# A hybrid attention and pooling layer on one Trainium2 core: the gate and pooled-channel projection by seven products of quarters in macro tiles 1 to 7, with x read already turned

## The chip, the cores and the metric

The kernel runs on one core of a Trainium2 chip, in one launch. The metric is the device time of that launch in microseconds (us). Before the change the median of 3 runs was 1232.03 us (1231.07 to 1233.27). Engines are named as in the profile: PE is TensorE (matrix products), PEld its weight loads, DVE is VectorE, ACT is ScalarE, POOL is GpSimd, SP is SyncE, whose queue issues all DMAs of this kernel.

## The reference, cut to what matters

x is 4096 tokens by 1024 channels, float32. One layer:

```
h    = RMSNorm(x) * pre_norm_g
q, k, v, g_a, u_p, g_p = split(h @ w_in)       # widths 512, 128, 128, 512, 512, 512
a    = banded_attention(q, k, v) * silu(g_a)   # 8 query heads, 2 key heads, |i-j| <= 128, bias, sink
p    = multiscale_pool(u_p) * silu(g_p)        # centred means over 2/4/8/16 tokens minus the token,
                                               # a 128x128 map per group of 128 channels, a scale
out  = x + RMSNorm([a ; p] @ w_out) * post_norm_g
```

The change is about the 1536 columns g_p, g_a and u_p of the product h @ w_in.

## The kernel before, in words

Every float32 operand of a large product is split into two float16 halves, high and low, and a product is taken as three: high by high, low by high, high by low. All three accumulate in the same PSUM bank. Weights are scaled by powers of two ahead of the split, which the gates' scale factors undo.

**Two stages.** Stage A projects g_p, g_a and u_p with tokens in the free dimension, stage B does all the rest: q, k, v, scores, softmax, values, the gated product, the output product by seven products of quarters (already so in both kernels), and the residual. Stage A ends where the first k projection starts (528.8 us in the profile).

**Stage A** goes over 8 macro tiles (m) of 512 tokens, each with 12 weight tiles (si) of 128 columns: 0 to 3 are g_p, 4 to 7 g_a, 8 to 11 u_p. One call of mm(m, si) (L593) is 24 matmuls: 8 blocks of 128 channels by 3, each with 128x128 weights and 512 moving columns. Its PSUM bank is one of three in turn (bank, L79). What follows a tile is set in after (L604): for a gate a sigmoid on ACT (L497), a multiply on DVE (L502) and, for g_a, a store to DRAM (L506); for u_p an evacuation on ACT (L515), edges of 8 tokens copied to and from the neighbour (L522, L523), and one macro tile later the pooled means: 1 to 4 dependent sums on DVE (L535), one more step (L551), the gate's multiply on POOL (L558) and a store.

**x** comes in token order in four blocks of 128 per macro tile (L157). The square sum goes to ACT (L163), the row scale to POOL (L172, L176), the high half to ACT (L185), the low half to DVE (L188). A DMA then turns the halves so that channels lie on partitions (x_turn, L195). The turned tiles are also stored (L200) and read back in stage B.

**Weights.** Each weight tile is loaded (L216), multiplied by the pre-norm gain on DVE (w_fold, L223), squared on ACT (L251), partly summed on POOL (w_presum, L257), summed over partitions by a product with ones on PE (w_norm, L266), scaled (scale_pow, L117 to L132, then the reciprocal at L275), and split on ACT (w_high, L281) and DVE (w_low, L285). A weight tile of u_p is first multiplied by the map of its pooling group: u_load (L227), u_prod on PE (L236), u_fold on DVE (L244). This happens in macro tile 0 for the 12 tiles of stage A. In macro tiles 1 to 3 it happens for the 6 tiles of q, k and v, two per macro tile. Macro tile 4 takes the norm of w_out, tiles 5 and 6 its split into quarters and their sums and differences (wo_sum1, wo_sum2, wo_high, wo_low; L443 to L483). Raw weights lie in 6 slots of 128x1024 float32.

**Order.** All instructions of a stage are put into a list by due(t, function, ...) with a due time t written by hand (L636) and are issued, on each engine's own queue, in the order of t, ties in the order of the list. The due times fix this order and nothing else: at run time each instruction waits for what it reads and for what it overwrites, and whatever stands behind it on its engine's queue waits too. Before the products of macro tile 0 six products of a tile of ones keep PE busy (warm_up, L576). The first two weight tiles of macro tile 0 go block by block as x arrives (mm_block, L586).

Lines that the prediction also uses: L371 (eight rows of attention bias scaled and masked on DVE), L599 (the products of mm), L847 (the q and k projection of stage B), L883 (scores), L981 (the v projection).

Of the kernel before, what the change touches and what calls it, by code (L numbers as in the profile page):

```python
# [17 lines left out]
P = 128  # L18
# [38 lines left out]
H_SCALE = 2.0**10  # L57
# [3 lines left out]
QKV_EVAC = 2.0**-14  # L61
U_EVAC = 2.0**-15
GP_EVAC = 2.0**-31
GA_EVAC = 2.0**-45
# [4 lines left out]
def hybrid_layer(ctx: ExitStack, tc, io, out):  # L69
# [22 lines left out]
    wb_h = const.tile([P, 6, KT, P], F16, name="wb_h")  # L92
    wb_l = const.tile([P, 6, KT, P], F16, name="wb_l")
    bias = const.tile([P, NH, 3 * P], F32, name="bias")
# [3 lines left out]
    cg = const.tile([P, 8], F32, name="cg")  # L98
    invc = const.tile([P, NH], F32, name="invc")
# [9 lines left out]
    x_scr = dram.tile([NM, P, BPM, 2 * KT, P], F16, name="x_scr")  # L109
    yp_scr = dram.tile([NB, P, 4, P], F32, name="yp_scr")  # L110
    ga_scr = dram.tile([NB, P, 4, P], F32, name="ga_scr")
    w_scr = dram.tile([8, P, 2, HK, 512], F16, name="w_scr")

    def scale_pow(dst, n2, floor, top):
# [17 lines left out]
        nc.vector.tensor_scalar(out=dst, in0=m4, scalar1=2.0**63, scalar2=None, op0=ALU.mult)  # L132


    xpool = ctx.enter_context(tc.tile_pool(name="xpool", bufs=1))


    with ExitStack() as actx:
# [4 lines left out]
        wa_h = pa1.tile([P, 12, KT, P], F16, name="wa_h")  # L143
        wa_l = pa1.tile([P, 12, KT, P], F16, name="wa_l")
        edge = pa1.tile([P, 4, 16], F32, name="edge")

        x_t, x_n, x_p, rs_t, w_t, n2_t, sq_t = {}, {}, {}, {}, {}, {}, {}
        pw = pa1.tile([P, 4, P], F32, name="pw")


# [4 lines left out]
        def x_load(b):  # L155
            x_n[b] = pa.tile([P, D], F32, name=f"xn{b}", tag="xn", bufs=4)
            nc.sync.dma_start(x_n[b], io["x"][b * P : (b + 1) * P, :])  # L157

        def x_square(b, eng=None):
            junk = pa.tile([P, D], BF16, name=f"jk{b}", tag="sq")  # L160
            rs_t[b] = pa.tile([P, 1], F32, name=f"ssq{b}", tag="ssq", bufs=4)
            if eng is None:
                nc.scalar.activation(junk, x_n[b], AF.Square, scale=X_SQ, accum_out=rs_t[b])  # L163
            else:
                eng.tensor_tensor_reduce(
                    out=junk, in0=x_n[b], in1=x_n[b], scale=X_SQ**2, scalar=0.0,
                    op0=ALU.mult, op1=ALU.add, accum_out=rs_t[b],
                )

        def x_scale(b):  # L170
            s = rs_t[b]
# [3 lines left out]
            rs_t[b] = pa.tile([P, 1], F32, name=f"rs{b}", tag="rs", bufs=4)  # L175
            nc.gpsimd.tensor_tensor(out=rs_t[b], in0=s, in1=mhalf, op=ALU.pow)  # L176

        def x_high(b):
            m, i = divmod(b, BPM)
            if i == 0:  # L180
                pool = xpool if m % 2 else pa1
                x_t[m] = pool.tile([P, BPM, 2 * KT, P], F16, name=f"xt{m}", tag="xt")
            tag, bufs = ("wraw", W_BUFS) if b in (2, 3) else ("xp", 2)
            x_p[b] = pa.tile([P, 2, D], F16, name=f"xp{b}", tag=tag, bufs=bufs)
            nc.scalar.activation(x_p[b][:, 0], x_n[b], AF.Copy, scale=rs_t[b])  # L185

        def x_low(b):
            nc.vector.scalar_tensor_tensor(  # L188
                out=x_p[b][:, 1], in0=x_n.pop(b), scalar=rs_t.pop(b), in1=x_p[b][:, 0],
                op0=ALU.mult, op1=ALU.subtract,  # L190
            )

        def x_turn(b):
            m, i = divmod(b, BPM)
            nc.sync.dma_start(  # L195
                x_t[m][:, i], x_p.pop(b).rearrange("p a d -> p (a d)"), transpose=True
            )

        def x_store(m):
            nc.sync.dma_start(x_scr[m], x_t[m])  # L200

        def x_block(b, t):

            due(t, x_square, b)
            due(t + 1.2, x_scale, b)
            due(t + 2.2, x_high, b)
            due(t + 3.4, x_low, b)
            due(t + 4.7, x_turn, b)


        gg = pa.tile([P, KT, P], BF16, name="gg", tag="yt")
        gb = g_pre.rearrange("p (k o) -> p k o", o=1).to_broadcast([P, KT, P])

        def w_load(si, src):
            w_t[si] = pa.tile([P, KT, P], F32, name=f"wraw{si}", tag="wraw", bufs=W_BUFS)
            nc.sync.dma_start(w_t[si], src)  # L216
# [5 lines left out]
        def w_fold(si, eng=nc.vector):  # L222
            eng.tensor_tensor(out=w_t[si], in0=w_t[si], in1=gb, op=ALU.mult)  # L223

        def u_load(j):
            w_t["u", j] = pa.tile([P, D], F32, name=f"wut{j}", tag="wraw", bufs=W_BUFS)
            nc.sync.dma_start(w_t["u", j], io["w_uT"][j])  # L227

        def u_prod(j, half):

            wt = w_t["u", j]
# [8 lines left out]
        def u_fold(j, half):  # L240
            if half == 0:
                w_t[A_U + j] = pa.tile([P, KT, P], F32, name=f"wu{j}", tag="wraw", bufs=W_BUFS)
            ks = slice(half * 4, half * 4 + 4)
            nc.vector.tensor_tensor(  # L244
                out=w_t[A_U + j][:, ks, :], in0=w_t.pop(("up", j, half)), in1=gb[:, ks, :],
# [3 lines left out]
        def w_square(si):  # L249
            sq_t[si] = pa.tile([P, KT, P], BF16, name=f"sq{si}", tag="sq")  # L250
            nc.scalar.activation(sq_t[si], w_t[si], AF.Square)  # L251
# [9 lines left out]
        def w_norm(si, n, by=None):  # L261

            sq = sq_t.pop(si)
            n2_t[si] = psa.tile([P, P], F32, name=f"n2_{si}", tag="n2")
            for k in range(n):
                nc.tensor.matmul(  # L266
                    n2_t[si], ones16 if by is None else by[:, k, :], sq[:, k, :],
                    start=(k == 0), stop=(k == n - 1),
                )

        def w_scale(si):
            scale_pow(sc[:, si : si + 1], n2_t.pop(si), 1e-20, W_SCALE)
# [1305 lines left out]
```

## Time and profile before

| | us |
|---|---|
| median of the runs | 1232.03 |
| span of the profiled execution, first to last instruction | 1229.4 |
| macro tile 0 of stage A | 0 to 92.6 |
| macro tiles 1 to 7 | 92.6 to 528.8 |
| stage B | 528.8 to 1229.4 |
| PE busy | 1203.6 |
| DVE busy | 826.3 |
| ACT busy | 633.6 |
| POOL busy | 380.6 |

The profile is that of one execution; the median of the runs lies 2.6 us above its span, which holds what surrounds the first and last instruction and the spread of runs. A page gives busy time per engine, a timeline of 40 slices, the queues, the chain that ended last and the costliest groups of instructions, each by line, engine, operation, tile names, shapes and count, with busy time and mean duration. "Idle before, releaser" is the time in which the engine stood still just before these instructions, and who ended it. Views of the trace give the same for a stretch of time, a line or a tile, or the instructions in order of time. Matmuls overlap in their pipeline, so the duration of one (379 ns for 512 columns) is longer than the distance from start to start.

### The profile page before, as it was taken

What the parts mean: (1) busy time and instruction counts of PE and PEld (TensorE: products, weight loads), DVE (VectorE), ACT (ScalarE), POOL (GpSimd) and SP (SyncE); (2) the same over time, 40 slices, a digit from 0 to 9 for tenths busy, and PEclk for the clock granted to TensorE, in tenths of its full rate; (3) what the DMA queues carried; (4) which work ended last, traced back from release to release, by engine and by line L of the source; (5) the groups of instructions that cost most, each with busy time, mean ns of one, the idle gap of its engine ahead of it and who ended that gap; (6) DMA issues with size and microseconds to landing.
All of it is one profiled execution on the core that took longest, in us unless ns stands there. A gap on an engine that the chain in (4) does not pass through costs nothing. (4 is left out here: it accounts for less than half of the span.)

```text
span 1229.4 us, 22327 instructions
## 1 busy us (share of the span) xinstructions
PE 1203.6 (98%) x8677; PEld 700.4 (57%) x8678; DVE 826.3 (67%) x1722; ACT 633.6 (52%) x1346; POOL 380.6 (31%) x385
## 2 busy tenths in 40 slices
PE   5999999999999999999999999999999999999998
PEld 4644444444444444476666765766676676667653
DVE  6665354545666564437778778777877877787786
ACT  5553333333435351136666755666575566667663
POOL 1233131313621211201244335424433533443331
PEclk9999999999999999999999999999999999999999
DMA  9473647496758783266957757765875676786594
GB/s 238 168 196 105 186 140 180 143 213 205 198 192 234 239 244 112 60 229 135 278 141 197 174 132 189 197 166 149 197 183 128 187 196 167 145 198 155 126 269 120
DMA packets 338986, 218.59 MB, mean 178 GB/s; under 512 B 267024, under 2 KB 309648, under 8 KB 335168
## 3 DMA queue, kind: packets, MB, share of 16 engines
q1 hardware_dynamic: 338880, 217.17, 65.9%
q8 instruction: 68, 1.11, 0.4%
q14 instruction: 38, 0.31, 0.1%
HBM read 94.43 MB, written 57.18 MB: 123 GB/s over the span
## 5 line engine op out<-in xcount | busy, mean ns | idle before, releaser
L599 PE MATMUL a<-xt,wa_h 128*128 128x512 f16 x1504 | 449.2, 379 | 0.1
L599 PE MATMUL a<-xt,wa_l 128*128 128x512 f16 x752 | 285.0, 379 | 0.0
L599 PEld LDWEIGHTS <-wa_h 128*128 128x128 f16 x1504 | 147.1, 98 | 175.9
L915 ACT ACTIVATE p<-p,nm 128x385 f32<-128x385 f32 (+1 forms) x256 | 153.0, 599 | 57.2 <-POOL p L898 37.9
L945 DVE SCALAR_TENSOR_TENSOR pn<-p,rd,pn 128x384 f16<-128x384 f32 (+1 forms) x256 | 156.5, 658 | 26.3 <-ACT pn L937 25.7
L847 PE MATMUL aq<-xt,wb_h 128*128 128x256 f16 x1024 | 173.1, 273 | 0.3 <-DVE mo L1182 0.3
L1154 PE MATMUL ms<-wo,ys 128*128 128x512 f16 x720 | 162.7, 379 | 1.5 <-ACT pn L937 1.5
L904 DVE CUSTOM_DVE_ANT_0 p<-s,bias,nsink 128x384 f32<-128x384 f32 (+1 forms) x256 | 155.9, 664 | 1.3 <-PE s L883 1.0
L937 ACT ACTIVATE pn<-p,rd 128x384 f16<-128x384 f32 (+1 forms) x256 | 136.3, 597 | 23.7 <-ACT p L915 21.2
L847 PE MATMUL aq<-xt,wb_l 128*128 128x256 f16 x512 | 139.5, 272 | 0.0
L847 PEld LDWEIGHTS <-wb_h 128*128 128x128 f16 x1280 | 125.2, 98 | 24.9 <-issue 9.3
L558 POOL TENSOR_TENSOR yt<-yt,s 128x512 f32<-128x512 f32 x32 | 51.5, 1608 | 256.9 <-DVE yt L551 148.2
L599 PEld LDWEIGHTS <-wa_l 128*128 128x128 f16 x752 | 73.5, 98 | 87.2
L1154 PE MATMUL m<-wo,y 128*128 128x512 f16 x540 | 119.7, 379 | 0.6 <-POOL y L1060 0.4
L1154 PEld LDWEIGHTS <-ys 128*128 128x128 f16 x720 | 69.1, 98 | 84.5 <-issue 4.2
L497 ACT ACTIVATE s<-a,cg 128x512 f32<-128x512 f32 x62 | 42.2, 684 | 145.3 <-PE a L599 140.8
L502 DVE SCALAR_TENSOR_TENSOR s<-a,s 128x512 f32<-128x512 f32 x62 | 42.4, 687 | 104.8 <-ACT s L497 104.8
L1188 POOL TENSOR_TENSOR mo<-mo,gpost 128x512 f32<-128x512 f32 x39 | 64.5, 1655 | 87.8 <-ACT jkb L1177 86.7
L1154 PEld LDWEIGHTS <-y 128*128 128x128 f16 x540 | 51.4, 98 | 65.3 <-issue 4.4
L188 DVE SCALAR_TENSOR_TENSOR xp<-xn,rs,xp 128x1024 f16<-128x1024 f32 x32 | 49.6, 1551 | 53.4 <-ACT xp L185 53.3
L883 PE MATMUL s<-k_all,q 64*128 64x384 f16 (+2 forms) x912 | 72.9, 296 | 2.8 <-ACT q L836 1.4
L1025 PE MATMUL o<-pt,vv 128*64 128x256 f16 x1128 | 68.2, 274 | 1.2 <-DMA pt<-pn 1.1
(159 smaller groups left out, 1589.2 us busy)
## 6 DMA issues: line engine op xcount, KB each, us to landing
xn<-in_x SPq DMA_DIRECT2D x32, 512.0 KB, 4.3
x_scr<-xt SPq DMA_DIRECT2D x7, 2048.0 KB, 7.4
xt<-x_scr SPq DMA_DIRECT2D x14, 1024.0 KB, 7.5
xr<-in_x SPq DMA_DIRECT2D x28, 512.0 KB, 4.1
out<-xr SPq DMA_DIRECT2D x28, 512.0 KB, 3.7
ga_scr<-s SPq DMA_DIRECT2D x32, 256.0 KB, 2.9
yp_scr<-yt SPq DMA_DIRECT2D x32, 256.0 KB, 2.3
w_scr<-wop SPq DMA_DIRECT2D x32, 256.0 KB, 2.6
```

The source lines that it names most:

```text
L188: nc.vector.scalar_tensor_tensor(out=x_p[b][:, 1], in0=x_n.pop(b), scalar=rs_t.pop(b), in1=x_p[b][:, 0], op0=ALU.mult, op1=ALU.subtract,)
L558: nc.gpsimd.tensor_tensor(out=t, in0=t, in1=g_t.pop((m, A_GP + j)), op=ALU.mult)
L599: nc.tensor.matmul(a3, w[:, si, k, :], x[:, :, kk, :], start=(n == 0), stop=(n == 3 * KT - 1))
L847: nc.tensor.matmul(a3, w[:, j, k, :], x[:, :, kk, :], start=(n == 0), stop=(n == 3 * KT - 1))
L883: nc.tensor.matmul(s_ps[:, gg, c0:c1], q_t[u, half][a, qi, jj, tl : tl + P], k_all[a, ki, kc : kc + c1 - c0], start=(n == 0 and c0 == 0), ...
L904: nc.vector.tensor_tensor_reduce(out=p_t[b, half][:, hh, :nk], in0=s_t[b, half][jj][:, gg, :nk], in1=bias[:, h, lo : lo + nk], scale=negc[ ...
L915: nc.scalar.activation(p[:, hh, : nk + 1], p[:, hh, : nk + 1], AF.Exp, bias=nm_t[b, half][:, hh : hh + 1], scale=-1.0, accum_out=den_t[b, ...
L937: nc.scalar.activation(prob_view(b, half)[:, 0, i], p_t[b, half][:, i, :nk], AF.Copy, scale=rd_t[b, half][:, i : i + 1],)
L945: nc.vector.scalar_tensor_tensor(out=pn4[:, 1, i], in0=p_t[b, half][:, i, :nk], scalar=rd_t[b, half][:, i : i + 1], in1=pn4[:, 0, i], op0= ...
L1025: nc.tensor.matmul(o_ps[a, 2 * half : 2 * half + 2], v[:, vi, kt, a], pt[b, half][:, pi, g, :, i, :], start=(n == 0), stop=(n == last),)
L1154: nc.tensor.matmul(z_t[u, tag], y[:, k, yi, :], wo[o][:, wi, k, :], start=(n == 0 and acc is None), stop=(n == 3 * HK - 1), skip_group_che ...
L1188: eng.tensor_tensor(out=mo, in0=mo, in1=gpost[:, cs], op=ALU.mult)
```

## The change: seven products of quarters, and x from a turned copy

**The product.** For each of the three groups q (QU for u_p, QP for g_p, QG for g_a) of four weight tiles, the product of 1024 channels by 512 tokens is taken by seven products of quarters (Strassen's scheme in Winograd's form). The quarters of x are two halves of the channels by two halves of the tokens, those of the weights two halves of the channels by two pairs of weight tiles. One product is 4 blocks of 128 channels x 3 (high, low) x 2 weight tiles = 24 matmuls with 256 moving columns; a macro tile takes 7 x 3 of them. Macro tile 0 still takes the plain product (mm, mm_block), its two weight tiles in blocks being 0 and 2.

**Sums.** From the turned x, four sums and differences of quarters per macro tile (x_sum), and eight casts to high and low halves, on ACT and DVE. From the weights, four sums per pair of weight tiles (t_sums on DVE, then t_high on ACT and t_low on DVE), made once, in macro tile 0 and at the start of macro tile 1. Weight tiles are now prepared in pairs (si, si + 2) with one scale for both: pair_scale waits for both norms.

**After a product.** Partial results are kept from PSUM on ACT (keep), joined to later ones on DVE (join), and gated (gates on ACT, gate_mult on DVE or POOL). One quarter leaves the bank directly (direct_u, direct_gates, direct_mult). The same three banks take five results in a row in each macro tile; two more banks take the second.

**x.** In macro tiles 1 to 7 x is read in token order for the square sums alone, and from a turned copy (an input that was there before, unused) for its values. The row scales go through DRAM to be spread over partitions (rs_row) and are multiplied in on DVE (y_scale). The DMA turns remain in macro tile 0 only.

**Moves.** The raw weight slots, the turned x and the weights of q, k, v share memory now, so the halves of q, k and v are stored and read back (wb_store, wb_load), and the attention bias and the post-norm gain are loaded late in macro tile 7, the bias rows (bias_head) following there on DVE instead of in macro tile 4. All scales drop by a factor of two. Stage B is otherwise as it was.

The due times of the steps for the attention weights and w_out keep their place as twelfths of a macro tile. The diff, cut to its core:

```diff
         for j in range(6):
             m, i, si = 1 + j // 2, 2 + 5 * (j % 2), SB + j
             also(m, i - 2, (0.2, w_load, si, io["w_b"][j]))
             also(m, i, (2.0, w_fold, si), (3.3, w_square, si), (4.4, w_presum, si))
             also(m, i + 2, ("norm", si))
+        def raw_put(key):
+            raw_free.append(w_t.pop(key))
+            if raw_wait:
+                raw_load(*raw_wait.pop(0))
+        def raw_load(key, src):
+            if raw_free:
+                nc.sync.dma_start(raw_get(key), src)
+            else:
+                raw_wait.append((key, src))
...
+        def t_sums(s1, eng=nc.vector):
+            r1, r2 = raw_of(s1), raw_of(s1 + 2)
+            b11, b21, b12, b22 = r1[:, :512], r1[:, 512:], r2[:, :512], r2[:, 512:]
...
+            minus(t1, b12, b11)
+            minus(t2, b22, t1)
+            minus(b11, b22, b12)
+            minus(b21, b21, t2)
+            raw_put(s1 + 2)
...
+        def t_low(s1, i):
...
+            if i == 1:
+                raw_put(s1)
...
+        STEPS = (
+            ("A11", 0, "p1"), ("A12", 1, "c11"), ("S2", 4, "u2"), ("S1", 2, "u4"),
+            ("S4", 3, "c12"), ("S3", 5, "c22"), ("A22", 6, "c21"),
+        )
+        def product(m, op, q):
...
+            for k in range(HK):
+                for wi, xi in ((0, 0), (1, 0), (0, 1)):
+                    for c in range(2):
+                        nc.tensor.matmul(
+                            acc[:, c], wa[:, q, wi, slot * HK + k, c * P : (c + 1) * P], x[:, xi, k, :],
+                            start=(fresh and n == 0), stop=(n > 3 * 2 * HK - 3),
+                            skip_group_check=True,
+                        )
+                        n += 1
...
+        def after(m, op, q, t):
+            what = STEPS[op][2]
+            if what in ("p1", "u2", "u4"):
+                due(t, keep, m, q, what)
+                return
...
+                    due(t, direct_gates, m, q)
+                    due(t + 1.0, direct_mult, m, q)
...
+            if q == QU:
+                if h == 0:
+                    due(t + 0.8, u_edges, m, n)
+                    if m:
+                        pooling(m - 1, 2 * n, t + 1.0)
+                        pooling(m - 1, 2 * n + 1, t + 2.0)
...
+        SLOT = 5.2
+        PT = 2.64
+        OP = 3 * PT
...
+        for si, s, n, f, h, l in (
+            (0, 9.25, 10.4, 10.7, 13.3, 14.5), (2, 10.3, 11.5, 11.9, 14.4, 17.1),
+        ):
+            due(s, w_square, si)
+            due(n, w_norm, si, KT, gg, 0)
...
+        due(11.0, row_prod)
+        due(11.4, warm_up)
...
+        pairs = [0, 1, 8, 9, 4, 5]
...
+            if n + 3 < len(pairs):
+                w = pairs[n + 3]
+                for i in range(2):
+                    if w >= A_U:
+                        due(now[0] + 0.2 + 0.1 * i, u_load, w - A_U + 2 * i)
...
         for m in range(1, NM):
-            for i, si in enumerate([8, 9, 10, 11, 0, 1, 2, 3, 4, 5, 6, 7]):
...
+            macro_x(m, t0)
+            for op in range(7):
+                for q in (QU, QP, QG):
+                    i = (3 * op + (QU, QP, QG).index(q)) * 12 // 21
...
+                    due(now[0], product, m, op, q)
+                    now[0] += PT
+                    after(m, op, q, now[0])
```

More of the change, by code (lines that the diff above doesn't have):

```diff
@@ L174, in x_scale @@
             )
[L175 to L185 removed]
+            nc.gpsimd.tensor_tensor(
+                out=r, in0=s, in1=mhalf if n == 1 else mhalf.to_broadcast([P, n]), op=ALU.pow
+            )
@@ new lines, in join, with gates @@
+        def join(m, q, b, part, n, h):
+            i = c_t[m, q, part]
+            c = cbig[:, i].rearrange("p (c t) -> p c t", c=2)
+            nc.vector.scalar_tensor_tensor(
+                out=dest(m, q, n, h) if q == QU else c, in0=acc_t[m, q, b], scalar=EV[q], in1=c,
+                op0=ALU.mult, op1=ALU.add,
+            )
+            if q == QU:
+                c_free.append(c_t.pop((m, q, part)))
+        def gates(m, q, part, n, h):
+            c = cbig[:, c_t[m, q, part]].rearrange("p (c t) -> p c t", c=2)
+            for i in range(2):
+                si = 4 * q + 2 * n + i
+                nc.scalar.activation(
+                    dest(m, q, n, h)[:, i], c[:, i], AF.Sigmoid, scale=cgs[:, si : si + 1]
+                )
@@ L730, in hybrid_layer @@
[L730 to L744 removed]
+        after0(0, 26.3)
```

832 lines of the change are left out of this document (569 added, 263 removed).

## Prediction

> **What bounds the kernel now.** I read the page first, then busy time by macro tile, then single instructions. The windows are macro tile 0, one ordinary macro tile (1 to 3 are alike), macro tiles 4 to 6, the last, and the attention stage with its start:
>
> ```profile
> span 1229.4 us, 22327 instructions
> ...
> 0.00:92.60 92.60, 79.37 (x565) 46.89 (x566) 59.16 (x133) 50.34 (x59) 21.81 (x31) 1.00 0.71 201
> ...
> 154.90:217.20 62.30, 62.30 (x293) 28.34 (x292) 29.43 (x50) 20.81 (x28) 14.45 (x16) 1.00 0.59 162
> ...
> 404.10:466.40 62.30, 62.30 (x290) 28.21 (x289) 37.09 (x50) 27.89 (x36) 11.12 (x12) 1.00 0.80 242
> 466.40:528.80 62.40, 62.40 (x291) 28.31 (x290) 26.51 (x52) 7.89 (x12) 10.39 (x10) 1.00 0.19 56
> 528.80:550.00 21.20, 18.88 (x202) 16.05 (x201) 8.03 (x24) 8.40 (x21) 0.19 (x1) 1.00 0.77 282
> 550.00:1229.40 679.40, 669.16 (x5886) 439.49 (x5883) 527.91 (x1185) 424.14 (x1068) 253.97 (x252) 1.00 0.69 174
> ```
>
> Columns: stretch, length, busy time of TensorE, weight loads, VectorE, ScalarE, GpSimd (with counts), granted clock, DMA share, GB/s. In macro tiles 1 to 7 TensorE is busy to the last hundredth and VectorE no more than 37.1 of 62.3: matmul columns set the time. Only macro tile 0 and the start of attention have gaps on TensorE. The span is 1229.4, the median of the runs 1232.0; I add the 2.6 between them at the end.
>
> **Term A, the products.** One projection tile (24 matmuls of 512 columns) and one pair of attention projections (48 of 256 columns, another weight each time, as in the new products), each alone:
>
> ```profile
> 66.43:71.61 5.18, 5.18 (x25) 2.26 (x24) 1.00 0.75 183
> 602.74:608.00 5.26, 5.26 (x48) 4.62 (x48) 1.00 1.13 239
> ```
>
> So 215.8 and 109.6 ns per matmul. A macro tile had 12 x 24 = 288, 62.16 us; it gets 7 x 3 x 24 = 504 of half the width, 55.23. Seven times 6.93 is **-48.5 us**. Weight loads are hidden at that rate in the second row. All else can only give this back.
>
> **Term B, macro tile 0.** It still runs the plain product, ten whole tiles after two in blocks, but prepares weights in pairs and builds four sums more of each pair. The order of instructions differs from the plan's intent in four places.
>
> ```profile
> 13.26 2.74 PE L576 MATMUL warm<-gg,ones 128*128 128x512 bf16 x6
> ...
> 28.69 2.02 PE L236 MATMUL wup<-pw,wut 128*128 128x128 f32 x16 [1.11 <-DMA wut<-in_w_uT]
> ...
> 35.73 0.38 PE L599 MATMUL a<-xt,wa_h 128*128 128x512 f16 x1
> ```
> ```profile
> 18.80 0.28 DVE L117 TENSOR_REDUCE m<-n 128x1 f32<-128x128 f32 x1
> ...
> 19.68 0.15 DVE L132 TENSOR_SCALAR sc<-m 128x1 f32<-128x1 f32 x1
> ...
> 37.98 1.28 DVE L285 SCALAR_TENSOR_TENSOR wa_l<-wraw,sc,wa_h 128x1024 f16<-128x1024 f32 x1
> 39.17 1.28 DVE L285 SCALAR_TENSOR_TENSOR wa_l<-wu,sc,wa_h 128x1024 f16<-128x1024 f32 x1
> ...
> 50.36 0.68 DVE L244 TENSOR_TENSOR wu<-wup,g_pre 128x512 f32<-128x512 f32 x1
> 50.96 0.15 DVE L275 RECIPROCAL isc<-sc 128x1 f32<-128x1 f32 x1
> ```
> ```profile
> 49.88 1.15 ACT L281 ACTIVATE wa_h<-wu,sc 128x1024 f16<-128x1024 f32 x1 [0.61 <-DVE sc L132]
> 51.80 1.06 ACT L251 ACTIVATE sq<-wu 128x1024 bf16<-128x1024 f32 x1 [0.76 <-DVE wu L244]
> ```
> ```profile
> 22.42 5.90 SPq L195 DMA_TRANSPOSE xt<-xp  x1
> ```
> ```profile
> DMA to landing us min/median/max: 4.4/5.5/7.9
> ```
> ```profile
> DMA to landing us min/median/max: 4.1/5.1/6.7
> ```
>
> The last two are the turned x blocks and the weight loads of the pooled channels. VectorE's pitch is 1.20 us at 1024 elements and 0.60 at 512, a scale takes 1.03 from its reduction to sc.
>
> First, the norm of weight tile 2 (w_norm) is queued behind the warm-up, which ends at 16.0, and the common scale needs it: scale at 18.1, high half 19.3, where the first block began at 15.8. The split of x blocks 2 and 3 queues behind, so the last turn is issued at about 26.9 instead of 22.4, lands at 32.4, and two blocks of a quarter tile (1.3 each) end at 35.2. Second, the six weight slots are full: the load of pooled tile 1 (u_load) waits until VectorE's sums of pair 0 (t_sums) free one, that of tile 3 until a low half of those sums (t_low) is done, and that low half stands behind the fold of tile 1 (u_fold) on VectorE, which needs the product (u_prod) of the first load. In a row: gates and low halves 3.0, fold 0.6, sums 1.9, load 5.1, half a product 1.0, fold and low half 1.2, load 5.1, product 2.0: 20 us. The first whole tile starts at about 55, not 35.7. Ten tiles (51.8) and norms (2.2) remain. Third, the norm of tile 10 stands behind the last product of pair 1, so tile 8 waits for scale, high and low half: 3.9. Fourth, VectorE has 54 us of work in the remaining 63, in order (20 sums and 20 low halves of 512 elements 24.0, 8 low halves of 1024 9.6, folds, scales and gates 13.5, x of macro tile 1 7): I count 5.4 more where tile 4 waits for its second load (1.6), tile 5 for its low half behind x's scaling (2.5) and tile 7 for the bank that the gate of tile 4 frees (1.3). End at 118.5 against 92.6: **+26**. Bounds: +17 with two loads at 4.1 and only the load chain and tile 8 counted, +32 with loads at 6.7 and a turn at 7.9.
>
> By the Trainium skill ("TensorE: Matmul & The Clock Gate", Part 1), an idle window of some 3.4 us halves TensorE's clock until it has been busy as long; the warm-up row agrees, 457 ns each against 215.8. No run here shows a pause of that length later; if the gaps between the pooled products do it, the sum would grow by an estimated 2 us.
>
> **Term C, norms of the attention weights in macro tiles 1 to 3.** Two per macro tile. On VectorE the fold (w_fold) comes after both pooled tiles (pool_tile) of its half, then the square on ScalarE, where the next gates are queued behind it, two partial sums on GpSimd and the norm on TensorE, where the next product is queued behind it.
>
> ```profile
> 353.69 0.71 DVE L535 TENSOR_TENSOR ws<-u 128x527 f32<-128x527 f32 x1
> 354.44 0.71 DVE L535 TENSOR_TENSOR ws<-ws 128x525 f32<-128x525 f32 x1
> 355.18 0.69 DVE L551 SCALAR_TENSOR_TENSOR yt<-ws,u 128x512 f32<-128x512 f32 x1
> 355.79 1.22 DVE L476 TENSOR_TENSOR wop<-wo_b,wop 128x1024 f16<-128x1024 f32 x1
> ```
> ```profile
> L257 POOL TENSOR_TENSOR sq<-sq x23: 669/1149/2051, 29.9 to 258.9; 128x512 bf16<-128x512 bf16 x13, 128x256 bf16<-128x256 bf16 x10
> ```
>
> A dependent sum has a pitch of 0.75, the last step 0.61. The second chain of a macro tile starts 1.2 after the first product of operand S4: pooled tiles 2 and 3 take 2.85 + 3.6, fold 1.2, square 1.1, partial sums 1.15 + 0.67 and hand-overs 0.2: 12.0. TensorE reaches the norm after three products, 7.9: it waits 4.1. The first chain (pooled tiles 0 and 1, 1.4 + 2.1) waits 0.9. GpSimd's gate of the one pooled tile also meets VectorE's sums of the other:
>
> ```profile
> 350.02 1.65 POOL L558 TENSOR_TENSOR yt<-yt,s 128x512 f32<-128x512 f32 x1 [19.07 <-DVE yt L551]
> 350.58 1.64 DVE L447 TENSOR_TENSOR wt<-wo_b,wt 128x512 f32<-128x512 f32 x1
> ```
>
> Beside it 1.64 instead of 0.69. I take half of that 0.95 per chain: 3 x (4.6 + 1.4) = **+18**; bounds +10 (pooled sums at a pitch of 0.60, no meeting) and +26 (each met, partial sums at 2.05).
> The Trainium skill ("SBUF — State Buffer", Who interferes with whom) says that a VectorE instruction with two inputs in SBUF and a GpSimd instruction that reads SBUF lock each other out for a whole instruction; the two rows agree. By its full price the sum would be 3 us higher here.
>
> **Term D, PSUM banks.** Each of three banks takes five results in a macro tile; TensorE may write again 5.3 us after a result is complete. After S4 the gate's multiply (direct_mult) on VectorE frees the bank, queued behind both pooled tiles: 1.2 + 6.4 + 0.7 = 8.3 against 7.9 in macro tiles 4 and 7. In 5 and 6 two subtractions and a low half of w_out (wo_sum1, wo_low) stand between, 2.5 more by the rows above: 2.9, with half a meeting 3.4 each. Together **+8**, bounds +2 and +13. ScalarE's keeps have slack.
>
> **Term E, x.** Reading x already turned takes 28 turns off SP's queue, and 28 splits off VectorE and ScalarE; TensorE had not waited for them, so that is worth 0. Added are four loads per macro tile (2 MB; the DMA share was 0.59 to 0.80) and the row of x's scales: written to DRAM, waited for on SP's queue with the last two loads queued behind it, read back broadcast. At about the loads' 4.1 us each way it takes 8 us, which is what lies between its due time and its use; squares that come late on ScalarE (C) delay it by 1 to 3. **+2**; 0, or +9 if it delays every chain of C and D.
>
> **Term F, start of attention.** Eight bias rows and the last pooled tiles now end on VectorE after the projection:
>
> ```profile
> L371 DVE SCALAR_TENSOR_TENSOR bias<-bias,invc,mask 128x384 f32<-128x384 f32 x8 | 7.9, 982 | 0.0
> ```
> ```profile
> 528.56 0.38 PE L599 MATMUL a<-xt,wa_h 128*128 128x512 f16 x1
> ...
> 540.23 0.28 PE L883 MATMUL s<-k_all,q 64*128 64x256 f16 x2 [0.75 <-ACT q L836]
> ```
>
> Scores began 11.4 us after the last product's pitch. From 6.9 before the end VectorE has 7.9 for bias, 9.9 for pooled tiles, 3.1 for joins and gates, then 1.4 for k, v and q: 15.4 after the end. **+4**, 0 to +6. Later stages keep instructions and order: 0.
>
> **Sum**: -48.5 + 26 + 18 + 8 + 2 + 4 = +9.5; span 1239, time **1241**. All low bounds together: -19.5; all high: +37.5.
>
> **Rivals.** *Faster:* VectorE's queue is ahead wherever TensorE is late, so only the load chain and the barest chains are left: +17, +10, +2, 0, +2 against -48.5, time 1214. It decides when the waits sum to under 46. For it speaks that VectorE's work still fits: per macro tile 16 passes over 1024 elements of x (19.5 at 1.22), 14 joins and gates of 512 (9.1), pooled tiles (10) and 7 to 15 for weights, 46 to 53 of 55 us; against it, that each chain starts from a product of its own macro tile, so an earlier queue doesn't shorten it. *Much slower:* every meeting with GpSimd at its full price (C +21, D +9) and the high bounds of B and E: -48.5 + 32 + 21 + 9 + 9 + 4, time 1258; VectorE is then the bound. For it speaks the 1.64 row, against it that the sums of L535 took 0.706 at the median, 2.736 at most:
> ```profile
> L535 DVE TENSOR_TENSOR ws<-ws x48: 694/706/2736, 104.7 to 511.9; 128x525 f32<-128x525 f32 x24, 128x521 f32<-128x521 f32 x16, 128x513 f32<-128x513 f32 x8
> ```
>
> *All hidden, as the due times say:* macro tile 0 ends at 90.5; 1185. The order of the loads speaks against it.
>
> **How the numbers follow.** Forecast 0.60 (1229 to 1252), faster rival 0.22, much slower 0.13, all hidden 0.05. The range 1212 to 1258 leaves out about 0.17. About 0.2% (2.5 us) is what a measurement tells from no change. Faster is the rivals' 0.27 less the part of the first near zero, 0.25; same 0.09, from the edges of the first rival and the forecast; slower 0.66.
>
> **What would show it.** First whole tile at about 55 and macro tile 1 at about 118; TensorE idle before the pooled products until the loads land; idle before norms in macro tiles 1 to 3, released by GpSimd, some 4 us in each second half and none in 4 to 7; a few us behind VectorE's gate multiply in 5 and 6; products at 2.63. Wrong if the first whole tile starts before 46 or if the norms are never waited for.

## The result, and the profile after

The changed kernel takes **1364.13 us** (median of 4 runs, 1361.21 to 1366.89) where the kernel before takes 1232.02 (4 runs, 1231.07 to 1233.27): a ratio of 1.107, 95% interval 1.105 to 1.109. The prediction said slower, 1241 us, range 1212 to 1258. The sign was right, and the size was missed by 123 us.

First the page of the changed kernel: the span, TensorE's line and the granted clock in 40 slices of 34 us.

```profile
span 1365.0 us, 25715 instructions
...
PE 1198.0 (88%) x10186; PEld 867.8 (64%) x10186; DVE 979.2 (72%) x1800; ACT 706.4 (52%) x1524; POOL 393.8 (29%) x363
...
PEclk9788989989897979889999999999999999999999
```

TensorE was busy 1203.6 us before and is busy 1198.0 now, although it has 48.5 us less to do, and its clock is no longer full in the first half of the span (each digit is a slice's granted clock in tenths, 9 for 90% or more). The next view has stretches as in the prediction: macro tiles 1 to 7, one a row, then the rest.

```profile
138.90:218.70 79.80, 61.08 (x509) 51.96 (x509) 56.25 (x74) 32.64 (x55) 16.06 (x12) 0.89 0.52 170
218.70:293.40 74.70, 59.12 (x511) 51.18 (x509) 48.06 (x61) 29.10 (x51) 17.21 (x13) 0.91 0.47 153
293.40:368.60 75.20, 59.28 (x510) 51.29 (x508) 47.80 (x61) 29.02 (x51) 17.20 (x13) 0.91 0.42 144
368.60:443.50 74.90, 59.95 (x508) 51.56 (x506) 44.29 (x68) 33.55 (x56) 28.76 (x17) 0.89 0.54 177
443.50:521.60 78.10, 60.09 (x506) 51.32 (x505) 55.98 (x68) 35.74 (x56) 11.20 (x9) 0.89 0.56 182
521.60:599.80 78.20, 60.46 (x506) 51.45 (x505) 56.15 (x61) 36.64 (x58) 12.02 (x9) 0.89 0.54 179
599.80:657.00 57.20, 55.38 (x506) 49.34 (x505) 36.03 (x47) 16.95 (x34) 11.15 (x8) 1.00 0.58 174
```

The columns are those of the prediction's first view: stretch, length, busy time of TensorE, weight loads, VectorE, ScalarE and GpSimd, granted clock, DMA share, GB/s. The last macro tile is what the products alone are worth: 57.2 us, TensorE busy 55.4, clock 1.00. It is also the only one that prepares no x for a next one. Each of the six others takes 75 to 80 us: 15 to 19 us of idle TensorE and 4 to 6 us more of busy time at a clock of 0.89 to 0.91. Macro tile 1 starts at 138.9 where the prediction had 118.5. The last product of stage A ends at 656.5 (before 528.8), and all that follows it takes 708.5 us (before 700.6).

The waits between 138 and 660 us (engine, line, releaser: us in total, times, longest) name who stood still for whom:

```profile
DVE ybig L279 <- DMA rb<-rs_scr: 75.8, 6, 17.9
...
PE n L389 <- POOL sq L376: 35.9, 6, 10.0
...
PE cl L902 <- ACT u L950: 32.5, 6, 7.1
...
PE cl L902 <- DVE gp L962: 24.2, 4, 7.8
```

VectorE waits once in each of macro tiles 1 to 6 (and once in macro tile 0) for the row of x's scales, which goes through DRAM (rs_row, L257 and L259; y_scale, L279). One macro tile in order of time shows how that reaches TensorE. First GpSimd, SyncE's queue, VectorE and ScalarE in macro tile 5, which starts at 443.5 (the time in brackets is the engine's idle time before the row and who ended it):

```profile
469.09 0.37 POOL L200 TENSOR_SCALAR ssq<-ssq 128x4 f32<-128x4 f32 x1 [2.54 <-ACT jk L191]
```
```profile
470.61 0.36 SPq L257 DMA_DIRECT2D rs_scr<-ssq  x1
479.47 0.33 SPq L259 DMA_DIRECT2D rb<-rs_scr  x1
```
```profile
473.55 1.23 DVE L687 TENSOR_TENSOR raw<-raw 128x1024 f16<-128x1024 f32 x1 [1.16 <-ACT raw L683]
484.85 2.36 DVE L279 TENSOR_TENSOR ybig<-ybig,rb 128x1024 f32<-128x1024 f32 x2 [10.07 <-DMA rb<-rs_scr]
...
494.53 0.70 DVE L775 TENSOR_TENSOR ws<-u 128x527 f32<-128x527 f32 x1
...
501.38 0.69 DVE L791 SCALAR_TENSOR_TENSOR yt<-ws,u 128x512 f32<-128x512 f32 x1
501.99 2.35 DVE L654 TENSOR_TENSOR raw<-raw 128x512 f32<-128x512 f32 x2
504.27 1.21 DVE L687 TENSOR_TENSOR raw<-raw 128x1024 f16<-128x1024 f32 x1
505.40 0.68 DVE L962 SCALAR_TENSOR_TENSOR gp<-ch,gp 128x512 f32<-128x512 f32 x1
```
```profile
486.11 1.04 ACT L285 CAST xt<-ybig 128x1024 f16<-128x1024 f32 x1 [6.00 <-DVE ybig L279]
491.27 1.15 ACT L651 ACTIVATE raw<-raw,rowsc 128x1024 f32<-128x1024 f32 x1 [4.12 <-DMA raw<-in_w_out]
...
493.26 0.59 ACT L950 ACTIVATE u<-ch 128x512 f32<-128x512 f32 x1
```

Then TensorE in the same stretch:

```profile
493.90 4.48 PE L902 MATMUL cl<-xt,wa 128*128 128x256 f16 x24 [6.58 <-ACT u L950]
506.13 15.65 PE L902 MATMUL cl<-xt,wa 128*128 128x256 f16 x120 [7.75 <-DVE gp L962]
521.62 8.02 PE L902 MATMUL ch<-xt,wa 128*128 128x256 f16 x72
```

The write of the row is issued 27 us after the start of the macro tile, not 20 as its due time says (x_loads at 1, the row 19 later), because the squares on ScalarE (L191) are late: GpSimd's row scale waits for the last of them. Its read can be issued only 8.9 us later and lands 5.4 us after that. VectorE is held for 10 us; the scaled x, the pooled tiles and the gate's multiply (L962) stand behind it in this order. ScalarE's cast of that x waits too, and behind it, with 4.1 us more of waiting for a load of w_out, stands the evacuation of the bank (direct_u, L950). So TensorE pauses twice, 6.6 and 7.8 us, and its first products behind each pause run slowly: 24 matmuls in 4.48 us, where such a row at full speed takes 2.78.

### The profile page after: what moved, and what is told of

It reads as the page before. It is cut to its first block, busy times and chain, and to the rows that moved or that the text cites. A ratio compares the mean times of both kernels' runs of the same rounds, so it can differ in the third digit from the quotient of the medians.

```text
span 1365.0 us, 25715 instructions
## 1 busy us (share of the span) xinstructions
PE 1198.0 (88%) x10186; PEld 867.8 (64%) x10186; DVE 979.2 (72%) x1800; ACT 706.4 (52%) x1524; POOL 393.8 (29%) x363
## 5 line engine op out<-in xcount | busy, mean ns | idle before, releaser
L902 PEld LDWEIGHTS <-wa 128*128 128x128 f16 x3528 | 357.0, 101 | 123.5 <-issue 71.2
L902 PE MATMUL ch<-xt,wa 128*128 128x256 f16 x2016 | 224.3, 273 | 7.3 <-ACT cbig L914 5.1
L1305 PEld LDWEIGHTS <-raw 128*128 128x128 f16 x1920 | 186.8, 98 | 39.5 <-issue 9.6
L902 PE MATMUL cl<-xt,wa 128*128 128x256 f16 x1008 | 135.4, 304 | 56.7 <-ACT u L950 32.5
L1374 ACT ACTIVATE p<-p,nm 128x385 f32<-128x385 f32 (+1 forms) x256 | 153.0, 599 | 57.2 <-POOL p L1357 38.0
L1305 PE MATMUL aq<-xt,raw 128*128 128x256 f16 x1536 | 173.1, 273 | 0.0
L1363 DVE CUSTOM_DVE_ANT_0 p<-s,ybig,nsink 128x384 f32<-128x384 f32 (+1 forms) x256 | 155.9, 665 | 1.4 <-PE s L1342 1.1
L279 DVE TENSOR_TENSOR ybig<-ybig,rb 128x1024 f32<-128x1024 f32 x28 | 33.4, 1221 | 88.3 <-DMA rb<-rs_scr 83.9
L1649 POOL TENSOR_TENSOR mo<-mo,ybig 128x512 f32<-128x512 f32 x39 | 64.8, 1661 | 87.5 <-ACT jkb L1638 86.3
L285 ACT CAST xt<-ybig 128x1024 f16<-128x1024 f32 x56 | 57.9, 1036 | 61.0 <-DVE ybig L279 48.1
L290 DVE TENSOR_TENSOR xt<-ybig,xt 128x1024 f16<-128x1024 f32 x56 | 69.5, 1249 | 14.7 <-ACT xt L285 14.7
L848 PE MATMUL a<-xt,wa 128*128 128x512 f16 x240 | 59.3, 406 | 18.4 <-ACT wa L425 16.8
```

The lines of the kernel that those rows point to most:

```text
L290: eng.tensor_tensor(out=o[:, w, 1], in0=y_view(i), in1=o[:, w, 0], op=ALU.subtract)
L848: nc.tensor.matmul(a3, weight(si, wi, k), xt[:, 0:2, k // HK, xi, k % HK, :], start=(n == 0), stop=(n == 3 * KT - 1),)
L902: nc.tensor.matmul(acc[:, c], wa[:, q, wi, slot * HK + k, c * P : (c + 1) * P], x[:, xi, k, :], start=(fresh and n == 0), stop=(n > 3 * 2 ...
L1305: nc.tensor.matmul(acc, w[:, j, k, :], x[:, k // HK, a, k % HK, :], start=(n == 0), stop=(n == 3 * KT - 1),)
L1363: nc.vector.tensor_tensor_reduce(out=p_t[b, half][:, hh, :nk], in0=s_t[b, half][jj][:, gg, :nk], in1=bias[:, h, lo : lo + nk], scale=negc[ ...
L1374: nc.scalar.activation(p[:, hh, : nk + 1], p[:, hh, : nk + 1], AF.Exp, bias=nm_t[b, half][:, hh : hh + 1], scale=-1.0, accum_out=den_t[b, ...
```

## The experiments

Theory 1: the row of x's scales is late and holds VectorE's queue. Norms, banks and x all come late by it, and the pauses drop TensorE's clock. Theory 2: the chains of norms and banks (terms C and D) are dear by themselves. Theory 3: the products of half width lower the clock by themselves. Times below are of one run each (the kernel before gave 1231.6 to 1232.2 beside them); differences are taken to the changed kernel's 1364.1 where no other kernel is named. The four runs of the changed kernel lie up to 5.7 us apart, so a difference of that size between two single runs tells nothing by itself.

### e1_no_row: no row through DRAM

```diff
-            nc.sync.dma_start(rs_scr[m].rearrange("(b p) -> p b", p=P), rs_t[m][:, 1])
-            rb_t[m] = pa1.tile([P, T], F32, name=f"rb{m}", tag="rb")
-            nc.sync.dma_start(
-                rb_t[m], rs_scr[m].rearrange("(o t) -> o t", o=1).to_broadcast([P, T])
-            )
+            rb_t[m] = rb_one        # set to 1.0 once, ahead of stage A
```

> The row of x's scales is not written to DRAM and read back; VectorE multiplies the turned x by a tile of ones that is set once (leaves out the scaling of x by rows in macro tiles 1 to 7). All else is as in the changed kernel, whose VectorE waited 84 us for the read of that row, seven times. Theory 1 (the row is late and holds VectorE's queue, so that norms, banks and x all come late, and the pauses drop TensorE's clock): no pause of TensorE over 5 us in macro tiles 1 to 6, its busy time per macro tile back from 59 to 61 to about 55.5, macro tiles 1 to 6 at 57 to 60 us each instead of 75 to 80, macro tile 0 about 12 us shorter: 1240 us (1230 to 1255). Theory 2 (the chains of norms and banks are dear by themselves, the row only fills idle time of VectorE): above 1330 us. Theory 3 (the clock drops because of the new products themselves, not because of pauses): pauses go but TensorE stays busy 59 to 61 us per macro tile: about 1270 us.

Measured **1298.3 us**: 65.8 less. Stretches of macro tiles 1, 2, 6 and 7:

```profile
130.20:200.80 70.60, 58.47 (x509) 50.92 (x509) 56.03 (x74) 32.69 (x55) 16.02 (x12) 0.95 0.56 188
200.80:265.30 64.50, 57.11 (x510) 50.37 (x508) 47.83 (x61) 29.03 (x51) 17.18 (x13) 0.97 0.51 172
...
465.80:531.80 66.00, 57.01 (x507) 49.94 (x506) 56.24 (x61) 36.65 (x58) 12.03 (x9) 0.97 0.64 208
531.80:588.40 56.60, 55.31 (x506) 49.28 (x504) 35.47 (x46) 16.96 (x34) 11.14 (x8) 1.00 0.59 176
```

This kernel leaves out the scaling of x. Macro tile 1 starts at 130.2, 8.7 sooner, and each of the six macro tiles is 8 to 12 us shorter. So the row costs 66 us, half of what was missed, and theory 1 holds for that half; the other half is still there. Its waits, by line (two lines higher than in the changed kernel: the norm L387, the gate's multiply L960):

```profile
PE n L387 <- POOL sq L374: 25.1, 6, 5.6
PE cl L900 <- DVE gp L960: 20.2, 4, 7.2
```

### e2_row_sooner and e11_row_sooner_base: the same with the row kept

```diff
-            x_loads(m + 1, t + 1.0)
+            x_loads(m + 1, t - 17.0)                          # e2
+            x_loads(m + 1, t - (19.0 if m > 1 else 9.0))      # e11, squares, scale and row 2 us further behind their loads
```

> The loads of x in rows, their squares, the scales and the row through DRAM are planned 18 us sooner for macro tiles 2 to 7 (that of macro tile 1 as it was); nothing is left out. Theory 1: VectorE waits for the row only once (8 us in macro tile 0), macro tiles 1 to 6 at 57 to 60 us each: 1255 us (1245 to 1270). Theory 2: within 15 us of the changed kernel's 1364. Theory 3: about 1285 us.

> The first edit of e4_pool_later alone: the row of x's scales sooner, pooled tiles and norms as in the changed kernel. Theory 1: like e2_row_sooner without its late start of macro tile 1: 1310 us (1303 to 1319), so that e4_pool_later's order of pooled tiles gave 12 us of its own.

Measured **1319.4** and **1312.9 us**. In e11_row_sooner_base VectorE waits for the row once, 7.0 us in macro tile 0, as theory 1 says (us and times, from the view of the tile rb):

```profile
  DMA rb<-rs_scr: 7.0, 1
```

Reading x sooner is enough to hide the round trip, and 51 us come back, although SyncE's queue still waits 63.1 us for the seven writes (63.5 in the changed kernel). So it is VectorE's wait that costs, not the wait on SyncE's queue. The 14.6 us left to e1_no_row lie in the start of macro tile 1 (7.6 later) and in macro tile 1 (7.0 longer). Theory 1's 1255 for e2_row_sooner was wrong for the reason that e1_no_row shows; nor did the milder shift remove the late start of macro tile 1 (TensorE still waits 7.5 us there for VectorE's multiply at L740, 9.4 in e2_row_sooner).

### e3_norm_later: the norms two products later

```diff
-            also(m, i + 2, ("norm", si))
+            also(m, i + 4, ("norm", si))
```

> The norms of the attention weights in macro tiles 1 to 3 stand two products later on TensorE's queue (their scale, halves and store with them); the row of x's scales stays as in the changed kernel. Theory 1: the pauses of 2.2 to 2.5 us in the first halves go (7 us in all), those of 9 to 10 us in the second halves only change their name, to a wait for VectorE's gate multiply as in macro tiles 4 to 6: 1357 us (1345 to 1366). Theory 2 (the wait for the norm is what costs the time): three times 10 + 2.4 us and the clock behind them, about 3 us each: 1319 us.

Measured **1372.8 us**, 8.7 more, a little outside theory 1's range on the far side of theory 2's 1319. The wait for the norm is gone from the list of TensorE's waits, and other names stand in its place:

```profile
PE ch L902 <- ACT cbig L914: 42.2, 11, 10.3
PE cl L902 <- DVE gp L962: 37.7, 7, 7.1
PE cl L902 <- ACT u L950: 20.0, 3, 7.8
```

So the 35.9 us that the changed kernel lists under the norm could not be won by moving the norm: all waits of TensorE in macro tiles 1 to 7 sum to 103.4 us there and to 105.7 here, under other names. A wait list names who came last, and with the row late several come late together.

### e10_order_alone, e4_pool_later, e5_norm_later_too, e8_pool_between: the order on VectorE's queue

```diff
-                        pooling(m - 1, 2 * n, t + 1.0)
-                        pooling(m - 1, 2 * n + 1, t + 2.0)
+                        pooling(m - 1, 2 * n, t + (6.5 if n else 1.0))        # e4, e5, e6 (on e11)
+                        pooling(m - 1, 2 * n + 1, t + (7.5 if n else 2.0))
+                        pooling(m - 1, 2 * n, t + (3.7 if n else 0.9))        # e8 (on e6), e10 (on the changed kernel)
+                        pooling(m - 1, 2 * n + 1, t + (8.1 if n else 2.8))
```

e5, e6, e8 and e10 also have e3's later norms.

> The changed kernel with only the pooled tiles put between the joins as in e8_pool_between and the norms two products later; the row of x's scales, its loads and macro tile 0 as in the changed kernel. Theory 1 (the late row holds VectorE's queue whatever stands behind it): VectorE still waits some 80 us for the row and TensorE 10 us or more per macro tile: 1345 us (1330 to 1362). Theory 2 (the order on VectorE's queue is the cause): the gain that it gives with the row in time, 35 us or more, comes here too: 1325 us or less.

Measured **1348.1 us**, 16.0 less and inside theory 1's range; the wait is where theory 1 puts it (VectorE, macro tile 0 included):

```profile
DVE ybig L279 <- DMA rb<-rs_scr: 94.3, 7, 18.5
```

> Two edits, nothing left out. The row of x's scales sooner as in e2_row_sooner (20 us for macro tiles 3 to 7, 10 for macro tile 2, and each square 2 us further behind its load). And the two pooled tiles of the second half of each macro tile planned 5.5 us later, behind the gate multiplies that free the banks and, in macro tiles 1 to 3, behind the fold of the attention weight. The first edit alone should give about 1305 us (e2_row_sooner lost some 14 us at the start of macro tile 1, where x's loads stood too early). Theory 1a (what is left of the pauses, 5 to 7 us per macro tile before the norm or the gate's bank, comes from the order on VectorE's queue: pooled tiles first): those pauses go, with the clock behind them 6 to 8 us in each of macro tiles 1 to 6: 1262 us (1250 to 1275). Theory 1b (VectorE has too much work, 48 to 56 of 65 us, so the wait only moves to the next join): 1295 to 1310 us.

Measured **1298.1 us**, 14.8 under e11_row_sooner_base. That lies in the range of theory 1b: the waits for the norm and the gate's multiply nearly vanish (24.1 to 8.2 us and 21.3 to 1.0), but 15.5 us of waits for the join of U and 7.6 for the other joins (L928) take their place. That VectorE has too much work, as 1b says, is not shown by it: the order alone could do the same.

> As e4_pool_later, and the norms of the attention weights two products later on TensorE's queue. Theory 1a: the 2 to 4 us before the first norm of macro tiles 1 to 3 go as well: 8 us under e4_pool_later. Theory 1b: no change.

Measured **1294.7 us**, 3.4 less, which single runs do not tell from nothing. By the traces macro tiles 2 and 3 are 4.0 and 2.7 us shorter and tiles 1 and 4 1.0 and 1.6 longer.

> As e6_first_macro_tile, with the four pooled tiles of each macro tile put one by one between the joins and gate multiplies that free banks (0.9, 2.8, 3.7 and 8.1 us behind the first product's end of their half), instead of two and two. e6_first_macro_tile still shows TensorE waiting 1.2 to 1.6 us for VectorE's join of P and 1.7 to 2.5 us for its join of U in each macro tile. If those are the pooled tiles ahead of the joins: some 3 us in each of macro tiles 2 to 7 go, 18 us: 1262 us (1257 to 1270). If VectorE has no room left, the waits move on: 1275 us or more.

Measured **1273.5 us**, 7.2 under e6_first_macro_tile, between the two. The gain is not where it was expected: macro tiles 2 and 3 take 59.6 and 59.0 us (57.1 and 58.9 in e6_first_macro_tile), while 2.7 us come from an earlier start of macro tile 1 and 3.1 from macro tile 1 itself. Tiles 2 and 3 have no wait for a norm or a gate's multiply; what remains there is a wait of about 2 us before the third product, for the last join of g_a, which stands behind the sums of x (L297) on VectorE. In 4 to 6, where w_out is scaled and split on the same queues, 63 to 64 us are left, with waits of 1 to 4 us for joins and for ScalarE's evacuations.

### e6_first_macro_tile, e7_pair_order_alone, e9_last_pair: macro tile 0

```diff
-        pairs = [0, 1, 8, 9, 4, 5]
+        pairs = [0, 1, 8, 4, 9, 5]          # e6 (on e5), e7 (on the changed kernel); e9 (on e8): 8, 4, 5, 9
-        x_loads(1, t1 - 50.0)
+        x_loads(1, t1 - 62.0)               # e6, e8, e9
-        due(11.4, warm_up)
+        due(12.0, warm_up)                  # e9
```

> The changed kernel with only the order of the pairs in macro tile 0 changed as in e6_first_macro_tile. Load chain as the cause of the late first whole tile: it starts at 42 to 47 us instead of 55; how much of that arrives at macro tile 1 tells whether the row of x's scales (read at 117 us) or VectorE's queue holds the end of macro tile 0: 9 us sooner if neither does (1355), nothing if one does (1364).

Measured **1356.9 us**: first whole tile at 44.5, macro tile 1 at 131.6, 7.3 sooner. The chain of two loads was real: the first whole tile starts 11.0 sooner, and 7.3 of that arrive at macro tile 1.

> As e5_norm_later_too, and in macro tile 0 the second pair of pooled channels comes one pair later in the order (so that its weights find a free slot before TensorE needs them) and x of macro tile 1 is read in rows 12 us sooner. If the two loads in a row and the late row of macro tile 1 cost what the prediction and the trace say: first whole tile at 42 to 47 us instead of 55, macro tile 1 from 139 to about 117, 20 us under e5_norm_later_too. If VectorE's work in macro tile 0 is the bound: first tile sooner, macro tile 1 not before 130.

Measured **1280.7 us**: first tile at 45.0, macro tile 1 at 128.5 and not 117, 14.0 under e5_norm_later_too. What holds the rest of macro tile 0 is not shown.

> As e8_pool_between, with the second pair of pooled channels last of all in macro tile 0 and the norm of weight tile 2 ahead of the warm-up on TensorE's queue. The waits of 6.0 and 2.6 us before the second pair's pooled products and 2 us of the first scale should go: macro tile 1 at about 117 us instead of 128, 1251 us. If VectorE's queue sets the end of macro tile 0, macro tile 1 stays later than 125.

Measured **1283.0 us**, 9.5 worse than e8_pool_between: refuted. The loads of the last pair now come at a worse place (7.4 and 10.3 us of idle TensorE ahead of its pooled products), and macro tile 1 starts at 133.7. The second of them is issued at 91.2, on SyncE's queue behind a wait of 9.2 us for the write of x's scales: the round trip again, on another queue.

### e12_fill_pauses: is it the pauses that lower the clock?

```diff
+        if m < NM - 1 and op == 5 and q != QG:
+            due(now[0], filler, m, "S4", 40 if q == QU else 64)   # matmuls into a free bank, read by nobody
```

> The changed kernel with matmuls whose result nobody reads (256 columns of operand S4 into a free bank) ahead of the two products before which TensorE pauses in macro tiles 1 to 6: 40 of them (4.4 us) before the first of operand S3 (pauses of 3.4 to 7.1 us), 64 (7.0 us) before the second (7.5 to 10 us). Nothing else changes, and nothing of the real work can come sooner by it. If the pauses are what lowers TensorE's clock (the product's matmuls behind them took up to 421 ns instead of 273, and TensorE's busy time was 28 us above that of six macro tiles at full clock): the rows behind the pauses at 273 ns, 20 to 28 us gained: 1340 us (1334 to 1348). If the products of half width lower the clock by themselves, or the pauses only absorb it: 1360 to 1370 us, the clock in the windows of macro tiles 1 to 6 no higher than 0.91.

Measured **1353.9 us**, 10.3 less for 70 us of useless products, between the two forecasts; the mean granted clock is 0.978 instead of 0.949. TensorE in macro tile 5:

```profile
480.42 4.53 PE L914 MATMUL fill<-xt,wa 128*128 128x256 f16 x40
486.50 2.78 PE L902 MATMUL cl<-xt,wa 128*128 128x256 f16 x24 [1.55 <-ACT u L959]
...
498.74 13.26 PE L902 MATMUL cl<-xt,wa 128*128 128x256 f16 x120 [2.48 <-DVE gp L971]
```

The same rows of the product (L902) took 4.48 and 15.65 us without the fillers, which are of half width too. So the pauses lower the clock, and theory 3 falls (macro tile 7 speaks against it too). Of 28 us of slow busy time only 10 came back: macro tiles 1 and 4 to 6 are about 3 us shorter each, tiles 2 and 3 not at all. There TensorE still waits 2.3 to 3.8 us ahead of each norm; why the norms come no sooner was not taken apart.

No version beats the kernel before. In the best, e8_pool_between, macro tile 1 starts at 125.8 (before 92.6), and macro tiles 1 to 7 take 436.9 us (before 436.2): the 48.5 us of the products are still given back in full, and 33 us of macro tile 0 and 8 behind the last product come on top.

## Why the prediction was wrong, step by step

The profiled span grew by 135.6 us where the sum had +9.5: macro tile 0 by 46.3 (predicted 26), macro tiles 1 to 7 by 81.4 (predicted -20.5: A, C, D, E), what follows the last product of stage A by 7.9 (predicted 4). The sign came out right, but +9.5 was a small remainder of terms of -48.5 and +58, so it rested on little.

**Term E is the step that failed.** It read "it takes 8 us, which is what lies between its due time and its use", priced the row at +2 and bounded it at +9. The runs show 66. Two things were wrong. The price of the trip was taken from the fastest of the loads of 512 KB, 4.1 us each way. The views of the DMA issues (KB each, median us to landing) show that the small write takes longer than a load of 256 times its size:

```profile
xn<-in_x SPq DMA_DIRECT2D x28, 512.0 KB, 4.9
...
rb<-rs_scr SPq DMA_DIRECT2D x7, 256.0 KB, 5.5
...
rs_scr<-ssq SPq DMA_DIRECT2D x7, 2.0 KB, 9.0
```

The row is written as 512 single float32, and the trip takes 14.5 us. The Trainium skill ("DMA: Bandwidth & Descriptors", Rules for kernel authors) says that a transfer whose last dimension is not contiguous becomes one descriptor per element. The trace agrees in the number of pieces: behind the write that is issued at 244.18 us, the DMA view of 245.0 to 245.5 counts 528 packets, all under 512 bytes, for the 512 elements. But the last of these packets starts at 245.44, and the write lands at 253.06, 7.6 us later, where the load of x in rows that is issued at 299.80 lands 0.4 us behind its last packet. So by these records the moving of the pieces is not what takes the 9.0 us, and no run shows what is. And the write starts 7 us after its due time. Due times fix an order, not a moment, as the section on the kernel says; the prediction used them as a moment. Nor do they lie 8 us from the use: the row is due at 20 and y_scale at 27, so that a trip of 14.5 would have been 7.5 late even with a write on time. The "+9 if it delays every chain of C and D" saw the mechanism, but a wait at the head of VectorE's queue is paid by the pooled tiles, folds, joins and gate multiplies behind it, in six macro tiles and once in macro tile 0 (macro tile 1 starts 8.7 sooner without it).

**Term A was right.** Macro tile 7 takes 56.6 us from its first product to the end of its last, 55.4 of them busy (predicted 55.23); a product at full clock lasts 2.62.

**Term B was right up to the first whole tile,** and too low behind it. Rows of TensorE in macro tile 0 of the changed kernel:

```profile
55.52 6.12 PE L848 MATMUL a<-xt,wa 128*128 128x512 f16 x24
...
73.86 0.61 PE L848 MATMUL a<-xt,wa 128*128 128x512 f16 x1 [6.36 <-ACT wa L425]
75.19 7.99 PE L848 MATMUL a<-xt,wa 128*128 128x512 f16 x23 [0.71 <-DVE wa L428]
...
124.48 0.61 PE L848 MATMUL a<-xt,wa 128*128 128x512 f16 x1 [10.46 <-ACT wa L425]
```

The first whole tile starts at 55.5, predicted 55, and e7_pair_order_alone shows that the two loads in a row are why. The wait of tile 8 was predicted at 3.9; it is 7.1 in two steps, and 2.9 more of slow clock in the next 23 matmuls (such a row takes 5.1 at full speed). Behind it lies a chain that the prediction had not followed: ScalarE's square of the next pair waits for a norm of TensorE that frees its buffer, with the high halves of the sums queued behind, and VectorE's low halves and the scale of tile 8 behind those. ScalarE's row in the same stretch:

```profile
67.36 1.06 ACT L370 ACTIVATE sq<-raw 128x1024 bf16<-128x1024 f32 x1 [4.35 <-PE n L389]
```

The 10.46 at 124 is the row again: the scale of the last pair stands behind y_scale on VectorE, which waited 8.1.

**Term C kept inside its bounds, term D did not.** With the row out of the way (e1_no_row) the norms are waited for 25.1 us against 18 predicted, bounds 10 to 26. The gate's multiply is waited for 20.2 us against 8, bounds 2 to 13: in the second half of macro tiles 5 and 6 pooled tiles, subtractions and a low half take VectorE 10.9 us ahead of it (494.53 to 505.40 in the rows of macro tile 5 above; 505.80 to 516.65 in e1_no_row), where the prediction counted 8.9, and in e1_no_row they start 1 us later than it assumed, behind a cast of x on ScalarE and its low half on VectorE. Macro tile 4, with a share of 0.4 in the prediction, waits 7.2 us. Waits at ScalarE's evacuations and at VectorE's joins, some 9 us, were in no term.

**The clock was in the prediction as a sentence beside the sum, worth 2 us in macro tile 0.** The busy time of macro tiles 1 to 6 is 27.7 us above six times that of macro tile 7 (16 in e1_no_row). The Trainium skill ("TensorE: Matmul & The Clock Gate", Part 1) puts the drop behind an idle window of some 3.4 us that runs freely. The traces agree for long pauses and differ for shorter ones: in macro tiles 1 to 7 of the changed kernel and of all experiments, the products' matmuls behind every pause over 3.3 us took up to 417 to 421 ns instead of 273, behind those under 1.9 they did not, and between the two both were seen (slow behind 1.97 us at 154.85 in the changed kernel, not behind 2.52 at 314.37). The error was to ask only whether the change makes such pauses in macro tile 0; every forecast wait of more than 3 us, like the 4.1 of term C, brings its own slow stretch.

**Term F** (+4, 0 to 6) measured 7.9. The work that it named is the cause, but at another place: bias rows and pooled tiles stand on VectorE ahead of the last join of U, for which TensorE waits 4.7 us before the first k projection, and the first products behind it run slowly (24 matmuls in 4.45 us instead of 2.78):

```profile
661.15 4.45 PE L1305 MATMUL kv<-xt,raw 128*128 128x256 f16 x24 [4.68 <-DVE u L928]
```

**How the rest divides.** e1_no_row has a span 67.0 us above the kernel before, where the sum without term E gives +7.5. The 60 us between them are 11.6 in macro tile 0, 7 in term C, 12 in term D, 9 of waits in no term, 16 of slow clock and 3 to 4 in term F.

**The rivals.** "Much slower" (1258) had VectorE as the bound by full meetings with GpSimd. VectorE did become the engine that all wait for, but by a wait at the head of its queue: it is busy 44 to 56 us of 75 to 80. The forecast and the other two rivals all took the row to be there in time.

What stays open: the 33 us that macro tile 0 still loses in e8_pool_between were not taken apart by runs, nor were the 63 to 64 us of its macro tiles 4 to 6; why e3_norm_later lost 8.7 us is not shown, and neither is what takes the 7.6 us between the row's last packet and its landing.

## What to carry to other kernels

When a change puts a DMA round trip between two instructions of a busy engine's queue, price it by a transfer of the same pattern and not by just any load, count from when its input is really ready and not from a due time, and charge the wait to everything queued behind it. Then ask of each wait on TensorE whether it is long enough to lower the clock, and add the slow stretch behind it. A wait list names the last one to come: here moving the named one (the norm) gained nothing, while removing the earlier wait it did not name gained 66 us.

## What the runs showed of the hardware that was not expected

A write of 2 KB in pieces of 4 bytes took 9.0 us to land where loads of 512 KB took 4.9 and 6.1, though its last packet had started 1.3 us after the issue. Some pauses of TensorE as short as 1.97 us were followed by matmuls of up to 417 ns instead of 273, others of up to 3.2 us were not. Matmuls of no use in the pauses made the kernel 10.3 us faster, by keeping the clock up.
